# Sums of the down projection's weights: made in DRAM by a queue of transfers instead of in SBUF by the seven passes

## The chip, the cores and the metric

One core of a Trainium2 chip runs the whole program. The time is that of one execution on the device, in microseconds (us). Three timed runs of the kernel before gave 1393.69 us in the median (1390.49 to 1396.89). The profile is of one further execution.

## The reference, cut to what matters

Two layers of a diffusion backbone work on 640 tokens: 512 latent tokens (tiles 0 to 3) and 128 context tokens (tile 4). Each layer has a mixing half and a SwiGLU half. The change lies in the last matrix product of the SwiGLU half, and the instructions that it moves past lie in the mixing half.

```python
def swiglu(h, w_gate_up, w_down):
    g, u = jnp.split(h @ w_gate_up, 2, axis=-1)
    return (jax.nn.silu(g) * u) @ w_down            # w_down: 2816 x 1024, float32
...
q_nope, q_rope, ckv, k_rope = mla_project(pd, ...)  # rmsnorm of parts of pd, then q and kv
p = jax.nn.softmax(s * scale, axis=-1)              # per head, 4 heads
...
x = x + gate2 * rmsnorm(swiglu(h2, w_gate_up, w_down), g_post_ffn)
```

## The kernel before, in words

**Precision.** A float32 operand is split into a high part (`fp32r`, made by ACT) and the rest (made by DVE). A product takes three matmuls, L227 to L229. Each weight tile goes DRAM, `raw` (a pool of three buffers), ACT, DVE, `w` (a pool of eight).

**The down projection.** `w_down` runs one level of a seven-product scheme: the inner dimension is halved (e = 0, 1) and so are the output columns (h = 0, 1). Four blocks of weights, each 2816 x 1024 / 4, and three sums of them are needed. Each block comes in six groups g: five of 512 KB and one of 256 KB. The seven passes stand in the order p1, p2, p5, p6, p3, p7, p4, and each goes over the six groups. In the kernel before, p1 loads block (0,0) into buffers `V` and uses it, then POOL issues an accumulating transfer that adds block (0,1) to `V` in SBUF (L1079), so that p5 finds a sum there; p5 adds a further block for p6, p6 one for p4, and p7 adds two blocks in a `raw` buffer. So each layer has 24 loads by SP (L1076, L1083) and 24 accumulating transfers by POOL.

**The order.** Program order is written out with a planner: `clk` counts estimated matmul time, `bg` is a list of steps that are put between matmuls at a given spacing, and `spawn`ed tasks wait a stated time. After that, a scheduler takes the program and puts the instructions of each engine in an order of its own: what is free of dependences may be moved far ahead of its place in the program. On the chip each engine works through its own order, one instruction after the other; a wait holds all that is queued behind it on that engine.

**POOL in the mixing half.** POOL has small jobs that others need: the reciprocal root of every rmsnorm (`rsq`: `rs` at L248/L250, `rt` at L252). For `pd_chain`, DVE multiplies `pdt` by `rt` (L696), TensorE transposes `pdt` (L240), and the results feed queries and keys. In `keys`, POOL writes the rotary rows of `kT` (L744, L745). In `scores`, POOL scales the probabilities of every second head, `P` (L810), and TensorE then transposes `P` (L240). `ada_sum` adds up modulation sums with matmuls (L346), copies them by ACT to `s`, waits a planned time, and transposes `s` (L240).

Of the kernel before, what the change touches and what calls it, by code (L numbers as in the profile page):

```python
# [131 lines left out]
class Trunk:  # L132
# [227 lines left out]
    def queue_ada_v(self, l, r):  # L360
# [5 lines left out]
        def step(half, k):  # L366
# [11 lines left out]
            if k == 7:  # L378
                self.spawn(self.ada_sum(mod, mc, half, acc, 1.10), 5.66)
# [665 lines left out]
    def w_down(self, l, src, hid, gg, nxt):  # L1045
# [13 lines left out]
        V = [None] * 3  # L1059
# [10 lines left out]
        def vg(g):  # L1070
            return V[g // 2][:, (g % 2) * 1024 : (g % 2) * 1024 + cnt(g) * 512]

        def into(g, e, h):
            if V[g // 2] is None:
                V[g // 2] = self.W()
            nc.sync.dma_start(out=vg(g), in_=dram(e, h, g))  # L1076

        def add(dst, e, h, g):
            nc.gpsimd.dma_start(out=dst, in_=dram(e, h, g), accum_op=ALU.add)  # L1079

        def fresh(g, e, h):
            r = self.raw()[:, 0 : cnt(g) * 512]
            nc.sync.dma_start(out=r, in_=dram(e, h, g))  # L1083
            return r

        def wsplit(g, s):
            w = self.wp.tile([128, 2, 1024], R, tag="w", name=self.nm("w"))
            n = cnt(g) * 512
            self.split(w[:, 0, :n], w[:, 1, :n], s)
            return w  # L1090
# [17 lines left out]
        def run(make, outs, tail=0, first=None, then=None):  # L1108


            kept = []
            for g in range(NG):
                h, w = first if first and g == 0 else make(g)
# [61 lines left out]
        def p1(g):  # L1175
            into(g, 0, 0)
            w = wsplit(g, vg(g))
            add(vg(g), 0, 1, g)
            h = xsplit(g, [x(g, 0)[:, :, A4]])
            self.tt(d(g), x(g, 1)[:, :, D4], x(g, 0)[:, :, D4], ALU.subtract)  # L1180
            return h, w
# [6 lines left out]
        def p2(g):  # L1188
            w = wsplit(g, fresh(g, 1, 0))
# [14 lines left out]
        def p5(g):  # L1204
            w = wsplit(g, vg(g))
            add(vg(g), 1, 1, g)
# [6 lines left out]
        def p6(g):  # L1213
            w = wsplit(g, vg(g))
            add(vg(g), 1, 0, g)
# [9 lines left out]
        def p3(g):  # L1225
            w = wsplit(g, fresh(g, 1, 1))
# [9 lines left out]
        def p7(g):  # L1236
            r = fresh(g, 0, 1)
            add(r, 1, 1, g)
            w = wsplit(g, r)
# [8 lines left out]
        def p4(g):  # L1248
            return xsplit(g, [x(g, 1)[:, :, B4]]), wsplit(g, vg(g))
# [91 lines left out]
    def run(self):  # L1341
# [4 lines left out]
        for l in range(L):  # L1346
# [9 lines left out]
            nxt = None  # L1356
            if l + 1 < L:
                mod1, q = self.queue_ada_w(l + 1, 0)
                self.bg, self.bg_last = [(6.6, f) for f in q], self.now + 12.0
# [7 lines left out]
            pre = self.w_down(l, x, hid, gg, nxt)  # L1367
# [42 lines left out]
```

## Time and profile before

| | |
|---|---|
| median of three runs | 1393.69 us |
| profiled execution | 1388.35 us, of which the span is 1386.5 us |
| PE busy | 1336.1 us (96%) |
| DVE / ACT / POOL busy | 1023.8 / 692.4 / 152.8 us |
| DMA | 203.68 MB: 179.25 MB by SP's queue (q1), 23.07 MB by POOL's (q0) |

A busy PE is not PE at its peak, since matmuls overlap; what an engine waits for says more. A row of the timeline has a start in us, a duration in us, the engine, the line, the operation with output and inputs, the number of instructions merged, and in brackets the idle time before it with what ended it.

### The profile page before, as it was taken

The page shows a single profiled execution, that of the slowest core. Times are in us where ns is not written, and L with a number is a line of the kernel's source. Part 1 is how long each engine was busy: PE and PEld are TensorE (multiplying, and loading weights), DVE is VectorE, ACT ScalarE, POOL GpSimd, SP SyncE. Part 2 cuts the span into 40 slices and gives each one's busy share as a digit, 9 for nine tenths or more (in the row PEclk, how much of TensorE's full clock was granted, in tenths as well). Part 3 has the DMA queues.
Part 4 walks back from the last instruction along what each step waited for, and adds up shares of the span by engine and source line. Part 5 has one row for each costly group of instructions (what it writes and reads, how often), then busy time and mean ns, then how long its engine had stood idle before and what let it go on. Part 6 is the DMA issues. An engine that isn't in the chain of part 4 may idle for free.

```text
span 1386.5 us, 21414 instructions
## 1 busy us (share of the span) xinstructions
PE 1336.1 (96%) x8188; PEld 1202.3 (87%) x8188; DVE 1023.8 (74%) x1794; ACT 692.4 (50%) x1398; POOL 152.8 (11%) x186
## 2 busy tenths in 40 slices
PE   5899999999999999999899899999999999999996
PEld 2789978899999999888688798778999999998885
DVE  3789476599988985777788956757977777665956
ACT  4543275565544454455673324746644444444734
POOL 1101121110000000121221101302000000010220
PEclk9999999999999999999999999999999999999999
DMA  9555247243333333778565623553223222365983
GB/s 374 170 178 185 89 140 245 104 169 108 122 122 107 122 121 125 176 143 193 171 213 170 197 88 122 175 207 123 76 92 92 80 88 77 107 177 126 184 200 119
DMA packets 57974, 203.68 MB, mean 147 GB/s; under 512 B 7488, under 2 KB 8384, under 8 KB 56848
## 3 DMA queue, kind: packets, MB, share of 16 engines
q1 hardware_dynamic: 50960, 179.25, 38.9%
q0 software_dynamic: 6912, 23.07, 9.5%
q8 instruction: 64, 1.05, 0.3%
q14 instruction: 38, 0.31, 0.1%
HBM read 191.61 MB, written 10.68 MB: 146 GB/s over the span
## 4 chain that ended last, share of the span: by engine, by line
PE 73%; DMA 9%; DVE 7%; issue 5%; ACT 3%; POOL 1%; POOLq 0%; DVEq 0%; ACTq 0%; SPq 0%
PE ps L227 23%; PE ps L229 22%; PE ps L228 22%; DMA raw<-in_w_dn 4%; PE ps L240 3%; DVE w L217 2%; DVE acc L377 2%; DMA raw<-in_ada 2%; PE ps L284 2%; ACT w L211 1%; DMA raw<-in_w_out 1%; PE ps L829 1%; POOL rt L252 1%; DMA raw<-in_w_s 1%; POOL rs L250 1%
## 5 line engine op out<-in xcount | busy, mean ns | idle before, releaser
L217 DVE TENSOR_TENSOR w<-raw,w 128x512 fp32r<-128x512 f32 (+2 forms) x220 | 198.0, 905 | 99.9 <-ACT w L211 98.6
L211 ACT ACTIVATE w<-raw 128x512 fp32r<-128x512 f32 (+2 forms) x220 | 175.5, 801 | 179.0 <-PE ps L229 82.2
L227 PE MATMUL ps<-T,w 128*128 128x320 f32 x640 | 198.5, 310 | 0.0
L229 PE MATMUL ps<-T,w 128*128 128x320 f32 x640 | 197.8, 309 | 0.0
L228 PE MATMUL ps<-T,w 128*128 128x320 f32 x640 | 197.7, 309 | 0.0
L227 PE MATMUL ps<-b,w 128*128 128x320 f32 x608 | 188.1, 309 | 0.0
L228 PE MATMUL ps<-b,w 128*128 128x320 f32 x608 | 187.9, 309 | 0.0
L229 PE MATMUL ps<-b,w 128*128 128x320 f32 x608 | 187.9, 309 | 0.0
L227 PE MATMUL ps<-w,hs 128*128 128x512 f32 x396 | 156.4, 395 | 8.0 <-ACT hs L211 6.7
L229 PE MATMUL ps<-w,hs 128*128 128x512 f32 x396 | 155.5, 393 | 3.0 <-DVE hs L217 3.0
L228 PE MATMUL ps<-w,hs 128*128 128x512 f32 x396 | 155.3, 392 | 0.0
L211 ACT ACTIVATE w<-sw 128x512 fp32r<-128x512 f32 x160 | 96.3, 625 | 77.4 <-PE ps L229 65.3
L211 ACT ACTIVATE s<-ps 128x320 f32<-128x320 f32 (+2 forms) x148 | 65.3, 442 | 126.6 <-PE ps L229 106.2
L214 DVE TENSOR_TENSOR s<-ps,s 128x320 f32<-128x320 f32 (+1 forms) x144 | 68.5, 481 | 75.7 <-PE ps L229 75.4
L227 PEld LDWEIGHTS ps<-T,w 128*128 128x128 f32 x640 | 120.1, 188 | 2.1 <-issue 1.7
L228 PEld LDWEIGHTS ps<-T,w 128*128 128x128 f32 x640 | 120.1, 188 | 0.0
L229 PEld LDWEIGHTS ps<-T,w 128*128 128x128 f32 x640 | 120.1, 188 | 0.0
L227 PEld LDWEIGHTS ps<-b,w 128*128 128x128 f32 x608 | 114.1, 188 | 0.4 <-ACT s L211 0.3
L228 PEld LDWEIGHTS ps<-b,w 128*128 128x128 f32 x608 | 114.1, 188 | 0.1
L229 PEld LDWEIGHTS ps<-b,w 128*128 128x128 f32 x608 | 114.1, 188 | 0.0
L217 DVE TENSOR_TENSOR w<-sw,w 128x512 fp32r<-128x512 f32 x160 | 106.0, 684 | 5.1 <-ACT w L211 3.2
L227 PEld LDWEIGHTS ps<-w,hs 128*128 128x128 f32 x396 | 75.1, 190 | 25.3 <-ACT hs L211 8.0
(236 smaller groups left out, 2848.0 us busy)
## 6 DMA issues: line engine op xcount, KB each, us to landing
raw<-in_w_gu SPq DMA_DIRECT2D x88, 512.0 KB, 3.5
raw<-in_ada SPq DMA_DIRECT2D x64, 512.0 KB, 4.5
raw<-in_w_dn SPq DMA_DIRECT2D x30, 512.0 KB, 3.6
wk<-in_w_dn POOLq DMA_DIRECT2D x30, 512.0 KB, 5.6
ada<-in_ada SPq DMA_DIRECT2D x8, 1024.0 KB, 15.5
raw<-in_w_out SPq DMA_DIRECT2D x16, 512.0 KB, 4.1
wk<-in_ada SPq DMA_DIRECT2D x8, 1024.0 KB
xs<-work SPq DMA_DIRECT2D x15, 512.0 KB, 4.8
```

Source lines behind the costliest of these rows:

```text
L211: self.nc.scalar.activation(out, in_, f, **kw)
L214: self.nc.vector.tensor_tensor(out, x, y, op=op)
L217: self.nc.vector.tensor_tensor(lo, src, hi.bitcast(F32), op=ALU.subtract)
L227: mm(out, lh, rh, start=start, stop=False, skip_group_check=more)
L228: mm(out, lh, rl, start=False, stop=False, skip_group_check=more)
L229: mm(out, ll, rh, start=False, stop=stop, skip_group_check=more)
L240: self.nc.tensor.transpose(out, in_, self.ident)
L250: self.nc.gpsimd.tensor_scalar(r, ms, EPS, None, op0=ALU.add)
L252: self.nc.gpsimd.tensor_tensor(r2, r, self.mhalf[:, :n], op=ALU.pow)
L284: self.nc.tensor.matmul(ps[32 * j : 32 * j + 32, :], self.cond[:, k, :], s, start=start, stop=stop, tile_position=(0, 32 * j))
L377: nc.vector.scalar_tensor_tensor(acc[:, s], raw, c, acc[:, s], op0=ALU.mult, op1=ALU.add)
L829: self.nc.tensor.matmul(ps[64 * e : 64 * e + 64, :], lhs[e], rhs[e], start=start, stop=stop, tile_position=(0, 64 * e))
```

## The change

A new function, `queue_sums`, makes four arrays `v[0]` to `v[3]` of sums per layer in DRAM. POOL issues all of it: 12 copies of weights DRAM to DRAM, 12 accumulating transfers on these, then six copies and six accumulating transfers for `v[1]`, and six and six for `v[3]`: 48 transfers per layer, 96 in all. The steps go into `bg` beside gate and up, spaced over 210 us of planner time. The seven passes load what they need with SP from the weights or from `v`, through `raw`, 42 loads per layer; `run` now makes the operands of group g + 1 before the matmuls of group g. Besides, `ada_sum` in the mixing half plans 6.0 us in place of 1.10 us before its transposes.

```diff
@@ -376,7 +376,7 @@
                 else:
                     nc.vector.scalar_tensor_tensor(acc[:, s], raw, c, acc[:, s], op0=ALU.mult, op1=ALU.add)
             if k == 7:
-                self.spawn(self.ada_sum(mod, mc, half, acc, 1.10), 5.66)
+                self.spawn(self.ada_sum(mod, mc, half, acc, 6.0), 5.66)
 
         return mod, [lambda h=h, k=k: step(h, k) for h in range(2) for k in range(8)]
 
@@ -1042,7 +1042,34 @@
             fast(j, cur, prep(j + 1, ops) if j + 1 < NJ else None)
         return hid
-    def w_down(self, l, src, hid, gg, nxt):
+    def queue_sums(self, l):
+        nc, a = self.nc, self.a
+        v = [[self.dp.tile([128, 1040], F32, tag=f"v{i}{g}", name=self.nm("v"))[:, 0 : (2 if g < 5 else 1) * 512] for g in range(6)] for i in range(4)]
+        def dram(e, h, g):
+            return a["w_dn"][l, e, h, g] if g < 5 else a["w_dt"][l, e, h]
+        def copy(i, g, s):
+            nc.gpsimd.dma_start(out=v[i][g], in_=s)
+        def add(i, e, h, g):
+            nc.gpsimd.dma_start(out=v[i][g], in_=dram(e, h, g), accum_op=ALU.add)
+        todo = []
+        for g in range(6):
+            todo.append(lambda g=g: [copy(0, g, dram(0, 0, g)), copy(2, g, dram(0, 1, g))])
+        for g in range(6):
+            todo.append(lambda g=g: [add(0, 0, 1, g), add(2, 1, 1, g)])
+        for i, (e, h) in ((1, (1, 1)), (3, (1, 0))):
+            for g in range(6):
+                todo.append(lambda g=g, i=i: copy(i, g, v[0 if i == 1 else 1][g]))
+            for g in range(6):
+                todo.append(lambda g=g, i=i, e=e, h=h: add(i, e, h, g))
+        return v, todo
+    def w_down(self, l, src, hid, gg, vs, nxt):
@@ -1067,23 +1093,9 @@
         def dram(e, h, g):
             return a["w_dn"][l, e, h, g] if g < 5 else a["w_dt"][l, e, h]
-        def vg(g):
-            return V[g // 2][:, (g % 2) * 1024 : (g % 2) * 1024 + cnt(g) * 512]
-
-        def into(g, e, h):
-            if V[g // 2] is None:
-                V[g // 2] = self.W()
-            nc.sync.dma_start(out=vg(g), in_=dram(e, h, g))
-
-        def add(dst, e, h, g):
-            nc.gpsimd.dma_start(out=dst, in_=dram(e, h, g), accum_op=ALU.add)
-
-        def fresh(g, e, h):
-            r = self.raw()[:, 0 : cnt(g) * 512]
-            nc.sync.dma_start(out=r, in_=dram(e, h, g))
-            return r
-
-        def wsplit(g, s):
+        def wsplit(g, src):
+            s = self.raw()[:, 0 : cnt(g) * 512]
+            nc.sync.dma_start(out=s, in_=src)
             w = self.wp.tile([128, 2, 1024], R, tag="w", name=self.nm("w"))
             n = cnt(g) * 512
             self.split(w[:, 0, :n], w[:, 1, :n], s)
@@ -1108,9 +1120,10 @@
         def run(make, outs, tail=0, first=None, then=None):
-            kept = []
+            kept, ready = [], first or make(0)
             for g in range(NG):
-                h, w = first if first and g == 0 else make(g)
+                h, w = ready
+                ready = make(g + 1) if g + 1 < NG else None
                 if g >= NG - tail:
                     kept.append((g, h, w))
                 else:
@@ -1173,9 +1186,7 @@
         b4 = [self.PS(), None]
         def p1(g):
-            into(g, 0, 0)
-            w = wsplit(g, vg(g))
-            add(vg(g), 0, 1, g)
+            w = wsplit(g, dram(0, 0, g))
             h = xsplit(g, [x(g, 0)[:, :, A4]])
             self.tt(d(g), x(g, 1)[:, :, D4], x(g, 0)[:, :, D4], ALU.subtract)
             return h, w
@@ -1186,7 +1197,7 @@
         later.append(lambda: [self.act(cc[:, 0, p, :], bA[p]) for p in range(2)])
         def p2(g):
-            w = wsplit(g, fresh(g, 1, 0))
+            w = wsplit(g, dram(1, 0, g))
             return xsplit(g, [x(g, 1)[:, :, A4]]), w
         go(p2, [(bC[0], 0, True, True), (bC[1], 128, True, True), (b4[0], 256, False, True)])
@@ -1202,8 +1213,7 @@
         later.extend(lambda t=t: left(t) for t in (0, 1, 4))
         def p5(g):
-            w = wsplit(g, vg(g))
-            add(vg(g), 1, 1, g)
+            w = wsplit(g, vs[0][g])
             return xsplit(g, [d(g)[:, :, 128:384]]), w
         go(p5, [(bB[0], 0, True, True), (bB[1], 128, True, True)])
@@ -1211,8 +1221,7 @@
         later.append(lambda: [self.act(cc[:, 1, p, :], bB[p]) for p in range(2)])
         def p6(g):
-            w = wsplit(g, vg(g))
-            add(vg(g), 1, 0, g)
+            w = wsplit(g, vs[1][g])
             s = d(g)[:, :, 128:384]
             nc.vector.scalar_tensor_tensor(s, s, -1.0, x(g, 0)[:, :, 0:256], op0=ALU.mult, op1=ALU.subtract)
             return xsplit(g, [s]), w
...
@@ -1234,9 +1243,7 @@
         later.extend(lambda p=p: end(p) for p in range(2))
         def p7(g):
-            r = fresh(g, 0, 1)
-            add(r, 1, 1, g)
-            w = wsplit(g, r)
+            w = wsplit(g, vs[2][g])
             h = self.Q([2, 2, 384], R, "hs")
             k = cnt(g)
             s = self.S()[:, 0 : k * 256].rearrange("p (k n) -> p k n", k=k)
@@ -1246,7 +1253,7 @@
             return h, w
         def p4(g):
-            return xsplit(g, [x(g, 1)[:, :, B4]]), wsplit(g, vg(g))
+            return xsplit(g, [x(g, 1)[:, :, B4]]), wsplit(g, vs[3][g])
         early = []
         steps = run(p7, [(bA[0], 0, None, True), (bA[1], 128, None, True), (b4[1], 256, False, True)], 2, None, lambda: early.append(p4(0)))
@@ -1354,9 +1361,11 @@
             x = self.dp.tile([NT, 128, D], F32, tag="xs", name=self.nm("xs"))
             pre = self.w_out(l, src, x, ys, gg, mod2, last)
             nxt = None
+            vs, qs = self.queue_sums(l)
             if l + 1 < L:
                 mod1, q = self.queue_ada_w(l + 1, 0)
-                self.bg, self.bg_last = [(6.6, f) for f in q], self.now + 12.0
+                qs = [x for k in range(max(len(q), len(qs))) for x in (*q[k : k + 1], *qs[k : k + 1])]
+            self.bg, self.bg_last = [(210.0 / len(qs), f) for f in qs], self.now + 12.0
             hid = self.gate_up(l, pre)
             self.drain_bg()
             gg = self.gates(gate, 1)
@@ -1364,7 +1373,7 @@
                 h = self.new_h()
                 src = self.dp.tile([NT, 128, D], F32, tag="xs", name=self.nm("xs"))
                 nxt = (mod1, h, src)
-            pre = self.w_down(l, x, hid, gg, nxt)
+            pre = self.w_down(l, x, hid, gg, vs, nxt)
             if l + 1 < L:
                 self.more_pd(l + 1)
                 self.mixer_start(l + 1)```

The instruction order shows where the scheduler puts all this. With n = 0 to 95 counted along POOL, transfers 0 to 47 belong to layer 0 and 48 to 95 to layer 1. `DMASW0` to `DMASW7` are the semaphores of POOL's transfers: transfer n raises number n mod 8. All 96 stand in POOL's order ahead of the first `P` scaling of layer 0. The first eight wait for nothing and stand first of all; later ones wait for a transfer issued six to eight places earlier.

POOL in layer 0, kernel before: the last two rmsnorms of `pd_chain` (`ms_544`, `ms_607`), then `kT_1249` and `kT_1250` (the rotary key rows) and the first `P`.

```order
L250 TENSOR_SCALAR rs_551<-ms_544 128x2 [waits Activation_49]
L252 TENSOR_TENSOR rt_553<-rs_551,mhalf 128x2 [waits Pool_49]
L250 TENSOR_SCALAR rs_611<-ms_607 128x2 [waits Activation_49]
L252 TENSOR_TENSOR rt_613<-rs_611,mhalf 128x2 [waits DVE_49,Pool_49]
L744 CAST kT_1249<-krT_283 64x640 [waits DVE_49,PE_49,Pool_49]
L744 CAST kT_1249<-krT_283 64x640
L745 TENSOR_TENSOR kT_1249<-krT_283,kT_1249 64x640 [waits Pool_49] x2
L744 CAST kT_1250<-krT_283 64x640 [waits DMAHW4_49,PE_49]
L744 CAST kT_1250<-krT_283 64x640
L745 TENSOR_TENSOR kT_1250<-krT_283,kT_1250 64x640 [waits Pool_49] x2
L560 COPY krT_6974<-ctx_6970 128x128 [waits DMAHW6_49,Pool_49]
L810 TENSOR_SCALAR P_1610<-P_1610,ri_1680 128x640 [waits DVE_49,Activation_49]
```

POOL in the changed kernel at the same rmsnorms; L1055 is a copy and L1058 an accumulating transfer, `v_28..` is layer 0 and `v_95..`, `v_96..` layer 1.

```order
L1058 DMA v_2867<-in_w_dn 128x1024 [waits DMASW6_49]
L250 TENSOR_SCALAR rs_551<-ms_544 128x2 [waits Activation_49]
L1058 DMA v_2868<-in_w_dn 128x1024 [waits DMASW7_49]
L252 TENSOR_TENSOR rt_553<-rs_551,mhalf 128x2 [waits Pool_49]
L1058 DMA v_2869<-in_w_dn 128x1024 [waits DMASW0_49]
L1058 DMA v_2870<-in_w_dt 128x512 [waits DMASW1_49]
L250 TENSOR_SCALAR rs_611<-ms_607 128x2 [waits Activation_49]
L1055 DMA v_9591<-in_w_dn 128x1024
L252 TENSOR_TENSOR rt_613<-rs_611,mhalf 128x2 [waits DVE_49,Pool_49]
```

The add into `v_2870` is transfer 47, and its wait on `DMASW1` is for transfer 41, the copy that it adds to. So `rt_613` now stands behind the landing of transfers 0 to 41, which are 24 copies and 18 accumulating transfers.

POOL in the changed kernel from the last transfers of layer 1 to the first `P`.

```order
L1055 DMA v_9614<-v_9602 128x512 [waits DMASW3_49]
L1058 DMA v_9609<-in_w_dn 128x1024 [waits DMASW4_49]
L1058 DMA v_9610<-in_w_dn 128x1024 [waits DMASW5_49]
L1058 DMA v_9611<-in_w_dn 128x1024 [waits DMASW6_49]
L1058 DMA v_9612<-in_w_dn 128x1024 [waits DMASW7_49]
L1058 DMA v_9613<-in_w_dn 128x1024 [waits DMASW0_49]
L1058 DMA v_9614<-in_w_dt 128x512 [waits DMASW1_49]
L744 CAST kT_1250<-krT_283 64x640 [waits DMAHW4_49,PE_49]
L744 CAST kT_1250<-krT_283 64x640
L745 TENSOR_TENSOR kT_1250<-krT_283,kT_1250 64x640 [waits Pool_49] x2
L560 COPY krT_7061<-ctx_7057 128x128 [waits DMAHW6_49,Pool_49]
L810 TENSOR_SCALAR P_1610<-P_1610,ri_1680 128x640 [waits DVE_49,Activation_49]
```

The copy into `v_9614` is transfer 89 and the add into it transfer 95. `kT_1250` and `P_1610` stand behind the landing of transfers 0 to 89, which are 48 copies and 42 accumulating transfers; `kT_1249` stands a little further ahead, behind transfer 79.

PE in layer 1, kernel before: the transposes of `s_7745`, the modulation sums that ACT copies out after the matmuls at L346, stand 11 matmuls behind those. The last eight of the 11 and what follows:

```order
L227 MATMUL ps_7722<-h_5789,w_7718 128x320
L228 MATMUL ps_7722<-h_5790,w_7718 128x320
L229 MATMUL ps_7722<-h_5789,w_7718 128x320
L227 MATMUL ps_7721<-h_5789,w_7718 128x320
L228 MATMUL ps_7721<-h_5790,w_7718 128x320
L229 MATMUL ps_7721<-h_5789,w_7718 128x320
L227 MATMUL ps_7722<-h_5789,w_7718 128x320
L228 MATMUL ps_7722<-h_5790,w_7718 128x320
L240 MATMUL ps_7756<-ident,s_7745 128x128 x4
L229 MATMUL ps_7722<-h_5789,w_7718 128x320
```

In the changed kernel the same transposes (of `s_7832`) stand 48 matmuls behind.

```order
L227 MATMUL ps_7809<-h_5863,w_7805 128x320
L228 MATMUL ps_7809<-h_5864,w_7805 128x320
L229 MATMUL ps_7809<-h_5863,w_7805 128x320
L240 MATMUL ps_7895<-ident,s_7832 128x128 x4
L227 MATMUL ps_7909<-h_5861,w_7906 128x320
```

They moved by 37 matmuls. The number of matmuls, and of ACT and DVE splits, is the same in both kernels.

## Rows read from the trace of the kernel before

**Rows 1.** The page: busy time and share of the span of each engine.
```profile
PE 1336.1 (96%) x8188; PEld 1202.3 (87%) x8188; DVE 1023.8 (74%) x1794; ACT 692.4 (50%) x1398; POOL 152.8 (11%) x186
```

**Rows 2.** Who PE waited for, 672 to 700 us: total, times, longest (us).
```profile
PE ps L227 <- ACT hs L211: 4.3, 1, 4.3
PE ps L229 <- DVE hs L217: 2.6, 3, 0.9
```

**Rows 3.** Who PE waited for, 1320 to 1386 us.
```profile
PE ps L227 <- ACT hs L211: 2.3, 1, 2.3
PE ps L227 <- ACT cc L211: 1.3, 1, 1.3
PE ps L229 <- DVE hs L217: 0.5, 1, 0.5
```

**Rows 4.** Who PE waited for, 720 to 870 us.
```profile
PE ps L240 <- ACT s L211: 6.0, 1, 6.0
```

**Rows 5.** Timeline of POOL, whole span: start, duration, operation.
```profile
12.40 0.57 POOL L252 TENSOR_TENSOR rt<-rs,mhalf 128x1 f32<-128x1 f32 x1
...
70.61 0.71 POOL L252 TENSOR_TENSOR rt<-rs,mhalf 128x2 f32<-128x2 f32 x1
...
161.29 1.49 POOL L744 CAST kT<-krT 64x640 fp32r<-64x640 f32 x2 [42.60 <-PE ps L228]
162.85 3.19 POOL L745 TENSOR_TENSOR kT<-krT,kT 64x640 fp32r<-64x640 f32 x2
166.11 0.29 POOL L560 COPY krT<-ctx 128x128 f32<-128x128 f32 x1
180.43 1.90 POOL L810 TENSOR_SCALAR P<-P,ri 128x640 f32<-128x640 f32 x1 [14.03 <-ACT V L211]
...
1340.95 0.87 POOL L1079 DMA_DIRECT2D raw<-in_w_dn  x1 [4.24 <-DMA raw<-in_w_dn]
1341.91 1.04 POOL L248 TENSOR_SCALAR rs<-mso 128x1 f32<-128x1 f32 x1
```

**Rows 6.** Timeline of all engines, 186 to 190 us: the first transposes of P.
```profile
188.76 1.25 PE L240 MATMUL ps<-ident,P 128*128 128x128 f32 x10
```

**Rows 7.** Who POOL waited for: total, times, longest (us).
```profile
POOL raw L1079 <- DMA raw<-in_w_dn: 39.9, 6, 14.6
```

**Rows 8.** DMA queues, 598 to 618 us: packets, MB, share of 16 engines.
```profile
q0 software_dynamic: 686, 2.55, 77.1%
```

**Rows 9.** DMA queues, 20 to 40 us.
```profile
q1 hardware_dynamic: 2130, 8.17, 101.9%
```

**Rows 10.** Windows: length, busy time (instructions) of each engine, granted clock, DMA share, GB/s.
```profile
0.00:71.00 71.00, 51.17 (x280) 34.93 (x281) 38.60 (x96) 34.15 (x83) 10.84 (x25) 1.00 0.70 266
71.00:180.00 109.00, 107.24 (x693) 95.94 (x692) 79.60 (x124) 39.96 (x79) 11.92 (x10) 1.00 0.47 152
0.00:180.00 180.00, 158.41 (x971) 130.87 (x972) 118.20 (x220) 74.11 (x162) 22.75 (x34) 1.00 0.56 197
```

**Rows 11.** Windows around the wait of rows 4.
```profile
795.00:800.00 5.00, 3.20 (x13) 3.20 (x14) 4.22 (x7) 1.54 (x2) 0.00 (x0) 0.50 0.74 226
800.00:810.00 10.00, 10.00 (x72) 10.00 (x71) 8.09 (x11) 3.24 (x6) 0.00 (x0) 0.98 0.53 179
```

More of the change, by code (lines that the diff above doesn't have):

```diff
@@ L1058, in w_down @@
         dd = [self.Q([3, 2, 384], F32, "dd") for _ in range(2)]
-        V = [None] * 3
         def x(g, e):
@@ L1225, in p3 @@
         def p3(g):
-            w = wsplit(g, fresh(g, 1, 1))
+            w = wsplit(g, dram(1, 1, g))
             s = d(g)[:, :, 128:384]
```

## The prediction, made before the changed kernel ran

> **What bounds the kernel now.** I read the page's busy times first: PE is busy 96% of the span [rows 1], so what can still be won is small, and what counts is what makes PE wait. Then I read who PE waited for in the two stretches of the down projection that have any such row: 6.9 us in layer 0 and 4.1 us in layer 1 [rows 2, 3], 11.0 us together. All else that the seven passes wait for lies beside matmuls. A third list holds one wait of 6.0 us for the modulation sums of layer 1 [rows 4]. Last comes POOL's timeline [rows 5]. POOL is idle most of the time, and for that reason its work is early: the last `rt` of layer 0's `pd_chain` is done at 71.3 us, `kT_1250` at 166.0, the first `P` at 182.3, and PE transposes that `P` at 188.76 [rows 6]. This is the schedule that the change touches, since the instruction order puts all 96 transfers ahead of that `P`.
>
> **What a wait on POOL does.** In the old down projection POOL stood 39.9 us in six waits for a load on which an accumulating transfer depended [rows 7]. After a wait of 4.24 us of that kind the transfer was issued at 1340.95, and the next `rs` followed at 1341.91, though nothing ties it to the transfer [rows 5]. So a transfer that waits holds the rmsnorms behind it.
>
> **Price of one transfer.** The mean size is (5 x 512 + 256) / 6 KB = 0.4806 MB. With POOL's queue alone at work, accumulating transfers moved 2.55 MB in 77.1% of 20 us, or 15.4 us [rows 8]: 165 GB/s, 2.91 us for the mean. SP's loads, back to back, moved 8.17 MB in 20.4 us of share [rows 9]: 401 GB/s, 1.20 us. An accumulating transfer in DRAM I price at 2.91 us, the row that it is nearest to; it cannot be under 2.40 (two streams read at 401 GB/s), it is 4.11 if reading the destination in DRAM costs a whole load on top (2.91 + 1.20), and 5.31 if writing it there costs as much again. A copy DRAM to DRAM is in no row. It reads one stream, as a load does, and writes to DRAM; it lies between 1.20 (a load) and 2.91 (an accumulation, which does all that a copy does and more). I take the middle, 2.05.
>
> The Trainium skill (DMA: Bandwidth & Descriptors, section on latency and other measured facts) gives 207 to 214 GB/s per direction for copies between HBM tensors. By it, a copy would be 2.29 us as an estimate, and the sum below 11.5 us longer. No row here shows it.
>
> **What else runs on the engines.** Up to 180 us the kernel moves 197 GB/s x 180 us = 35.5 MB, of it 266 x 71 = 18.9 MB in the first 71 us [rows 10]. At 401 GB/s that is 88 us, and 47 us of these in the first 71. In rows 9 the loads alone filled 101.9% of the 16 engines, so nothing is free beside them. I add the loads and the new transfers.
>
> The Trainium skill (same page, section "Issuing engines are not separate DMA queues") has it that transfers from SP and POOL end up on the same 16 engines and interleave. By that rule they add up; were the queues independent, the sum would lose the 88 us. Rows 9 agree as far as they go, since one queue alone fills all 16. The other way is the second rival.
>
> **The sum.** `rt_613` stands behind transfers 0 to 41, 24 copies and 18 accumulations: 47 + 24 x 2.05 + 18 x 2.91 = 149 us against 71. DVE's product with it, and behind that the weight splits, the loads and PE, all wait. `P_1610` stands behind 0 to 89, 48 copies and 42 accumulations: 88 + 48 x 2.05 + 42 x 2.91 = 88 + 98.4 + 122.2 = 308.6 us. Behind that come `kT_1250` (1.49 + 3.19), a copy (0.29) and `P` itself (1.90) [rows 5], 6.9 us: 315.5 us. PE wanted it at 188.76, so PE is 126.7 us late. The compute between these two points, 110 us, is shorter than the 160 us of transfers that lie there, so POOL still sets the end. From there on both kernels do the same work.
> - The issues themselves, 0.87 us each [rows 5], 90 of them 78 us, lie inside the 308.6 us of moving. Were the transfers quicker than the issues they would be the bound; they are not, at 1.20 us or more.
> - The clock: after the wait of 6.0 us PE had the lower level, 0.50 granted, over 5.0 us with 3.20 us busy [rows 11], which is 1.6 us lost at least. A long stall should end so too, at up to 5 us; I take 3. Restarts before the last are covered by POOL's lateness.
> - The down projection: 48 accumulating transfers in two layers go, and with them what PE waits for there: at most 11.0 us; some of these waits are for activations (`cc`, `hs`), not weights. I take 6, from 0 to 11. SP's 18 more loads per layer lie beside the passes at 1.20 us of engine time each, in place of 24 accumulations at 2.91.
> - The later transposes of `s`: 37 matmuls more ahead of them at 10 / 72 = 0.139 us [rows 11] hide 5.1 of the 6.0 us [rows 4]. I take 5, from 0 to 7.6 with the lower clock.
> - Splits, matmuls and evacuations are as many as before: 0. The lookahead by one group has eight `w` buffers for two in use; were it short of them, a pass would wait as now.
>
> 126.7 + 3 - 6 - 5 = 118.7 us. Against the profiled execution, 1388.35 + 118.7 = 1507 us; this stood 5.3 us under the median of the runs, 1393.69, so I forecast 1512 us.
>
> **Bounds.** Low prices: 88 + 48 x 1.20 + 42 x 2.40 = 246, so with the 6.9 and less 188.8 PE is 64 us late; less 18.6 for the gains at their most, nothing for the clock: 1439 us. High prices: 88 + 48 x 2.91 + 42 x 5.31 = 451, 269 us late, 5 for the clock, no gains: 1668 us; both at their highest together is unlikely.
>
> **Rivals.**
> 1. Both kinds are dearer in DRAM: a copy 2.91 us, an accumulation 4.11, since the destination is read from DRAM too, where before it lay in SBUF. For it: no row shows such a transfer. Against: in rows 8 the engines' own share, 77.1%, went with the low rate, so that reading two streams may already be the bound. 88 + 139.7 + 172.6 = 400, and 400 + 6.9 - 188.8 + 3 - 11 = 210 us: 1604 us.
> 2. The loads and POOL's transfers do not slow each other. For it: before 180 us the engines are 56% busy [rows 10], so there are gaps. Against: rows 9. Then 220.6 + 6.9 - 188.8 + 3 - 11 = 31 us: 1424 us.
> 3. The other side: POOL's chain is never late, the transfers being spread over a time in which POOL has nothing to do, and the gains remain. This decides at the first gate: 42 transfers in 70 us, or 1.67 us each, and 90 in 182 us, 2.02 us each, with nothing taken from the loads. The mean at my prices is 2.45 us; at the lowest it is 1.76 for the 90. Then 1388.35 + 5.3 - 11 = 1383 us. For it: POOL is busy 11% [rows 1].
> 4. The change doesn't do what it says. It speaks of gate and up; the instruction order has the transfers at the start of the program. That is no rival but the ground of the forecast; were they issued where they are written, rival 3's time would come out.
>
> **Chances.** Forecast 0.66, rival 1 0.15, rival 2 0.13, rival 3 (with 4) 0.06. The range, 1420 to 1640 us, takes in the low bound, rival 1, rival 2 and the high bound but for its last 28 us; it leaves out rival 3. This kernel's measurement can tell about 0.5%, or 7 us, from no change. Faster by more than that 0.04 (most of rival 3), within it 0.02, slower 0.94.
>
> **What the profile would show.** If I am right, PE's waits for DVE's `pdt` and for `kT` or `P` hold some 120 us before the end of layer 0's mixing, and POOL's longest waits are for DMA in the first 300 us; the DMA share there is near 1; the last `rt` of `pd_chain` comes at about 150 us and the first `P` of layer 0 at about 315; from there to the end it is as long as before, less about 11 us. The waits of rows 2 to 4 shrink. I am wrong in the price if the 96 transfers are through at 180 us or at 450; wrong in the mechanism if `P_1610` comes near 182 us, or if the lost time lies in the down projections.

## The result, and the profile after

The changed kernel took 1467.67 us in the median of four runs (1467.47 to 1469.24), the kernel before 1394.46 (four runs): a ratio of 1.052, 95% interval 1.0497 to 1.0543, slower. The forecast was 1512 us, so its direction and its place held, and its size was 44 us too long. The profiled execution took 1469.24 us. In two of the experiments below one run of four was slow (e5_half 1527.83 us, e10_early_copies 7500.69); their medians are of all four, 0.1 to 0.2 us above those of the fast runs, and ratios are of fast runs alone.

The page of the changed kernel, which answers to [rows 1]: busy time, then the granted clock and DMA share in 40 slices, then the two queues (packets, MB, share of 16 engines).

```profile
PE 1352.7 (92%) x8188; PEld 1219.8 (83%) x8188; DVE 1024.3 (70%) x1794; ACT 692.0 (47%) x1398; POOL 173.8 (12%) x234
...
PEclk9778879999999999999999999999999999999999
DMA  9999999563443343335556453355322222334553
...
q1 hardware_dynamic: 56144, 196.55, 40.3%
q0 software_dynamic: 13312, 46.14, 12.2%
```

All that is odd stands in the first seven slices, 257 us: DMA full, the granted clock down to 0.7. Windows of the changed kernel (columns as in [rows 10]) say the same in numbers: before, the engines were 0.70 and 0.47 busy in the first two.

```profile
0.00:71.00 71.00, 28.33 (x136) 14.86 (x136) 14.88 (x38) 17.52 (x32) 19.50 (x36) 0.89 1.00 337
71.00:180.00 109.00, 69.54 (x343) 60.71 (x343) 50.70 (x94) 29.73 (x77) 36.77 (x56) 0.83 1.04 302
180.00:260.00 80.00, 63.09 (x385) 59.43 (x386) 40.72 (x59) 17.92 (x34) 28.07 (x36) 0.82 1.02 273
260.00:300.00 40.00, 39.97 (x287) 31.65 (x287) 27.95 (x92) 24.28 (x71) 11.43 (x8) 1.00 0.49 159
```

POOL's timeline in the changed kernel, at the last rmsnorms of `pd_chain`, at `kT` and at the first `P`, answers to [rows 5].

```profile
101.81 0.23 POOL L250 TENSOR_SCALAR rs<-ms 128x2 f32<-128x2 f32 x1
104.66 0.90 POOL L1058 DMA_DIRECT2D v<-in_w_dt  x1 [2.62 <-issue]
105.27 1.05 POOL L252 TENSOR_TENSOR rt<-rs,mhalf 128x2 f32<-128x2 f32 x1
...
134.96 0.74 POOL L252 TENSOR_TENSOR rt<-rs,mhalf 128x2 f32<-128x2 f32 x1
...
228.53 1.49 POOL L744 CAST kT<-krT 64x640 fp32r<-64x640 f32 x2
...
257.48 1.49 POOL L744 CAST kT<-krT 64x640 fp32r<-64x640 f32 x2 [2.33 <-PE ps L228]
...
277.13 1.90 POOL L810 TENSOR_SCALAR P<-P,ri 128x640 f32<-128x640 f32 x1 [14.54 <-ACT V L211]
```

An `rs` is done at 102.04, but its `rt` follows at 105.27, since POOL stood idle for 2.62 us before a transfer between them, with which `rt` has nothing to do. The last `rt` comes at 134.96 instead of 70.61, the first `P` at 277.13 instead of 180.43. Who PE waited for in the first 290 us, the five longest of nine rows with 98.9 us together; none of the nine is for `kT` or `P`, and in the first 300 us of the kernel before the row of `pdt` had 1.8 us and that of `ada` 11.2:

```profile
PE ps L240 <- DVE pdt L696: 19.2, 4, 9.7
PE ps L240 <- ACT s L211: 18.0, 3, 13.4
PE ps L240 <- issue: 15.0, 1, 15.0
PE ps L228 <- DVE U L217: 11.6, 2, 6.9
PE ps L284 <- DMA ada<-in_ada: 10.9, 2, 9.2
```

And POOL's longest waits, 0 to 300 us. "issue" means that the profile names no releaser; L1058 are the accumulating transfers.

```profile
POOL v L1058 <- issue: 122.7, 42, 6.2
```

PE's waits in 808 to 958 us, the stretch of [rows 4], are below. In 761 to 789 and 1401 to 1468 us, the stretches of [rows 2, 3], no wait is listed any more.

```profile
PE ps L227 <- DVE ua L724: 2.7, 1, 2.7
PE ps L240 <- DVE work L438: 1.9, 1, 1.9
```

To see where each kernel wins or loses, I cut every span at four points of DVE's timeline: the start of its first and its last product into `hid` (the end of a step of gate and up) in either layer. Times in us; "middle" is layer 0's `w_down` and layer 1's mixing half, "end" is layer 1's `w_down`.

| | head | gate, up 0 | middle | gate, up 1 | end | span |
|---|---|---|---|---|---|---|
| before | 291.9 | 244.0 | 435.0 | 242.6 | 173.1 | 1386.5 |
| changed | 388.4 | 246.8 | 422.9 | 242.5 | 166.9 | 1467.5 |
| e2_none | 296.2 | 247.0 | 419.9 | 242.7 | 166.7 | 1372.5 |
| e1_paced | 297.7 | 256.5 | 422.1 | 248.5 | 166.9 | 1391.8 |
| e1_burst | 294.4 | 272.1 | 419.7 | 263.3 | 166.8 | 1416.4 |
| e7_copies | 294.2 | 255.3 | 419.8 | 242.6 | 166.8 | 1378.6 |
| e8_spread | 294.9 | 258.0 | 436.4 | 242.5 | 167.6 | 1399.4 |
| e6_small | 353.5 | 246.7 | 422.6 | 242.5 | 166.4 | 1431.7 |
| e4_mid | 379.3 | 247.9 | 420.8 | 242.6 | 166.7 | 1457.3 |
| e5_half | 359.3 | 245.7 | 420.5 | 242.5 | 166.8 | 1434.9 |
| e11_half_mid | 331.6 | 245.6 | 419.4 | 242.5 | 167.0 | 1406.2 |
| e10_early_copies | 365.4 | 246.1 | 422.8 | 242.5 | 166.7 | 1443.5 |
| e9_second | 294.6 | 245.7 | 429.1 | 244.2 | 166.9 | 1380.5 |

The changed kernel loses 96.5 us in the head and 2.8 in layer 0's gate and up (e2_none loses 3.0 there too, without a transfer; why stays open), and wins 12.1 and 6.2 us in the two stretches with a `w_down`.

### The profile page after: what moved, and what is told of

Same layout as the page of the kernel before. It is cut to its first block, busy times and chain, and to the rows that moved or that the text cites. A ratio compares the mean times of both kernels' runs of the same rounds, so it can differ in the third digit from the quotient of the medians.

```text
span 1467.5 us, 21508 instructions
## 1 busy us (share of the span) xinstructions
PE 1352.7 (92%) x8188; PEld 1219.8 (83%) x8188; DVE 1024.3 (70%) x1794; ACT 692.0 (47%) x1398; POOL 173.8 (12%) x234
## 2 busy tenths in 40 slices
DMA  9999999563443343335556453355322222334553
## 3 DMA queue, kind: packets, MB, share of 16 engines
q1 hardware_dynamic: 56144, 196.55, 40.3%
q0 software_dynamic: 13312, 46.14, 12.2%
q8 instruction: 64, 1.05, 0.3%
## 4 chain that ended last, share of the span: by engine, by line
issue 64%; PE 16%; DMA 9%; DVE 5%; POOL 4%; ACT 1%; SPq 0%; POOLq 0%; DVEq 0%; ACTq 0%
DMA raw<-in_ada 5%; PE ps L227 4%; PE ps L228 4%; PE ps L229 4%; DVE acc L377 2%; PE ps L240 2%; POOL rt L252 2%; PE ps L284 1%; DMA raw<-in_w_pd 1%; POOL v L1058 1%; DVE w L217 1%; PE ps L829 1%; DMA raw<-in_w_out 1%; POOL rs L250 1%; POOL rs L248 1%
## 5 line engine op out<-in xcount | busy, mean ns | idle before, releaser
L217 DVE TENSOR_TENSOR w<-raw,w 128x1024 fp32r<-128x1024 f32 (+2 forms) x268 | 252.4, 947 | 119.4 <-ACT w L211 118.0
L211 ACT ACTIVATE w<-raw 128x1024 fp32r<-128x1024 f32 (+2 forms) x268 | 222.2, 832 | 190.8 <-DMA raw<-in_w_b 71.2
L227 PE MATMUL ps<-T,w 128*128 128x320 f32 x640 | 198.7, 310 | 1.4 <-ACT s L211 1.2
L228 PE MATMUL ps<-T,w 128*128 128x320 f32 x640 | 197.8, 309 | 0.0
L229 PE MATMUL ps<-T,w 128*128 128x320 f32 x640 | 197.7, 309 | 0.0
L227 PE MATMUL ps<-b,w 128*128 128x320 f32 x608 | 188.4, 310 | 0.1
L229 PE MATMUL ps<-b,w 128*128 128x320 f32 x608 | 187.9, 309 | 0.0
L228 PE MATMUL ps<-b,w 128*128 128x320 f32 x608 | 187.8, 309 | 0.0
L227 PE MATMUL ps<-w,hs 128*128 128x512 f32 x396 | 154.4, 390 | 0.1
L228 PE MATMUL ps<-w,hs 128*128 128x512 f32 x396 | 154.1, 389 | 0.0
L229 PE MATMUL ps<-w,hs 128*128 128x512 f32 x396 | 153.9, 389 | 0.0
L211 ACT ACTIVATE w<-sw 128x512 fp32r<-128x512 f32 x160 | 96.0, 624 | 76.9 <-PE ps L229 64.6
L211 ACT ACTIVATE s<-ps 128x320 f32<-128x320 f32 (+2 forms) x148 | 65.2, 442 | 124.0 <-PE ps L229 100.4
L227 PEld LDWEIGHTS ps<-T,w 128*128 128x128 f32 x640 | 120.1, 188 | 4.0 <-ACT s L211 2.4
L214 DVE TENSOR_TENSOR s<-ps,s 128x320 f32<-128x320 f32 (+1 forms) x144 | 68.7, 483 | 78.0 <-PE ps L229 77.7
L228 PEld LDWEIGHTS ps<-T,w 128*128 128x128 f32 x640 | 120.1, 188 | 0.0
L229 PEld LDWEIGHTS ps<-T,w 128*128 128x128 f32 x640 | 120.1, 188 | 0.0
L227 PEld LDWEIGHTS ps<-b,w 128*128 128x128 f32 x608 | 114.1, 188 | 1.4 <-issue 0.8
L228 PEld LDWEIGHTS ps<-b,w 128*128 128x128 f32 x608 | 114.1, 188 | 0.1
L229 PEld LDWEIGHTS ps<-b,w 128*128 128x128 f32 x608 | 114.1, 188 | 0.0
L248 POOL TENSOR_SCALAR rs<-mso 128x1 f32<-128x1 f32 x20 | 10.0, 500 | 878.6 <-ACT work L211 878.5
L217 DVE TENSOR_TENSOR w<-sw,w 128x512 fp32r<-128x512 f32 x160 | 106.1, 685 | 5.3 <-ACT w L211 3.3
## 6 DMA issues: line engine op xcount, KB each, us to landing
raw<-in_w_gu SPq DMA_DIRECT2D x88, 512.0 KB, 3.6
raw<-in_ada SPq DMA_DIRECT2D x64, 512.0 KB, 6.6
v<-in_w_dn POOLq DMA_DIRECT2D x60, 512.0 KB, 10.8
raw<-v SPq DMA_DIRECT2D x40, 512.0 KB, 3.5
raw<-in_w_dn SPq DMA_DIRECT2D x30, 512.0 KB, 3.5
v<-v POOLq DMA_DIRECT2D x20, 512.0 KB, 9.4
raw<-in_w_out SPq DMA_DIRECT2D x16, 512.0 KB, 3.8
```

Source lines behind the costliest of these rows:

```text
L211: self.nc.scalar.activation(out, in_, f, **kw)
L214: self.nc.vector.tensor_tensor(out, x, y, op=op)
L217: self.nc.vector.tensor_tensor(lo, src, hi.bitcast(F32), op=ALU.subtract)
L227: mm(out, lh, rh, start=start, stop=False, skip_group_check=more)
L228: mm(out, lh, rl, start=False, stop=False, skip_group_check=more)
L229: mm(out, ll, rh, start=False, stop=stop, skip_group_check=more)
```

## Experiments

The kernel before was run again beside the experiments, with medians of 1393.1 to 1395.5 us; ratios are against it. Theory 1: the loss is in the head alone; the transfers add to the loads there, and POOL's order passes the delay on.

**Is it the place?** Each transfer is held behind the matmul recorded last where the program writes it (e1_paced), or all of a layer behind `w_out` (e1_burst); e2_none has none.

```diff
-            nc.gpsimd.dma_start(out=v[i][g], in_=s)
+            self.hold(nc.gpsimd.dma_start(out=v[i][g], in_=s), self.mark)   # e1_burst: start, taken at the head of queue_sums
```

> The changed kernel, with each of the 96 transfers that make the sums held behind the matmul last recorded where the planner puts it, so that they run through gate and up, and the head of the program has none. Theory 1 (loads and transfers share the DMA engines' time, and GpSimd's queue stands behind them; both only in the first 280 us): the 97 us by which the first P is late go, the 15 to 16 us that come back afterwards (97 us at P, 81 at the end) stay, 1394.5 - 15.7 = 1379 us, 1375 to 1387. Rival A (the delay comes from GpSimd's waits in its order alone): also 1379 here, since no work of the mixer stands behind a transfer. Rival C (the transfers' 180 us of engine time are paid wherever they run, by the loads of gate and up): no faster than before, 1394 or more.

> As the run with paced transfers, but all 48 transfers of a layer are held behind the last matmul of w_out, so that they run back to back at the start of gate and up, some 90 us for each layer. Theory 1: the 90 us of transfers and the loads of gate and up lie in a stretch where the engines were busy for a quarter to a half before, 1379 us, at most 5 us more where a burst and the loads together come to over 1.0; the rest as in the paced one. Rival C: 20 us or more above the paced one, since the loads of gate's first passes stand in the burst.

> The changed kernel without any of the 96 transfers: the four passes that load a sum load a plain block of the weights instead, so the sums are left out of the computation, and everything else stays. It is the floor. Theory 1: 1379 us, within 3 us of the paced one, since the transfers there are hidden; the first P stands where it stood before (180 us, within 3). If the transfers cost something in gate and up, this run is below the paced one by that. If the 15.7 us that came back after the first P came from elsewhere (later work having more slack because it started late), this run is at 1390 to 1395.

Measured: 1397.37 us (1.0013, 0.9992 to 1.0034), 1419.69 (1.0183) and 1375.61 (0.9862). The floor is 3 us under what was expected. All 92 us between it and the changed kernel hang on the transfers, and out of the head they cost 22 (paced) or 44 (burst). But 22 is not 0: theory 1 had said 1379. "In the head alone" fell, and rival A's 1379 with it. Rival C's numbers came true (1394 or more, the burst 20 or more above the paced run), though the price is 22 us and not 180. DMA queues in 350 to 400 us, e1_paced (accumulating transfers in pairs): queue rows as in [rows 8]; issue rows end with KB each and median us to landing.

```profile
q0 software_dynamic: 1734, 5.78, 61.4%
q1 hardware_dynamic: 1409, 5.24, 32.1%
...
raw<-in_w_gu SPq DMA_DIRECT2D x8, 512.0 KB, 9.9
```

The same stretch, e2_none:

```profile
q1 hardware_dynamic: 1696, 6.29, 36.6%
...
raw<-in_w_gu SPq DMA_DIRECT2D x8, 512.0 KB, 4.4
```

A weight load lands after 9.9 us instead of 4.4, later than it is needed. Who DVE waited for in 330 to 540 us of e1_paced (e2_none has 4.4 and 2.7 us in these rows), and who PE waited for in 275 to 540:

```profile
DVE sw L214 <- DMA raw<-in_w_gu: 10.1, 8, 2.5
...
DVE acc L410 <- DMA wk<-in_ada: 5.6, 2, 4.3
```

```profile
PE ps L227 <- DVE s L214: 6.4, 3, 3.7
```

In e2_none that row has 0.4 us. So PE waits for a DVE that had itself waited for loads.

**Is it the accumulating?** e7_copies drops it; e8_spread sends single transfers, layer 1's from layer 0's gate and up on.

```diff
-..., in_=dram(e, h, g), accum_op=ALU.add), self.mark)
+..., in_=dram(e, h, g)), self.mark)
```

```diff
+        if self.trk and self.now - self.trk_last >= self.trk[0][0]:   # in mm3; 5.2 us in layer 0, 13.0 us in layer 1
+            self.trk_last = self.now
+            self.hold(self.trk.pop(0)[1](), last.ins.name)
```

> The run with paced transfers (1397.4 us), with each of the 48 accumulating transfers made a plain copy of the same bytes, so that the sums are not sums; the count, the order and the holds stay. Theory 2, formed from the paced run (gate and up lost 9.5 us in layer 0 and 5.9 in layer 1 against the run without transfers, and in layer 0 nearly all of it in 350 to 400 and 442 to 488 us, where accumulating transfers ran, none where copies ran): the loss goes with the accumulations, about 1378 us, 1375 to 1383. Rival D (a load is delayed by any transfer of these bytes): the loss stays, or falls only in the ratio of the engines' time (1.2 us for a copy, 2.2 for an accumulation), 1388 to 1397.

> The changed kernel with all 96 transfers made one at a time behind matmuls: layer 0's one in 5.2 us of gate and up, layer 1's one in 13 us from there to layer 1's gate and up. It tries for the gain without the price. By theory 2 an accumulation alone delays a load by about its own 2.2 us, which a stretch with a load every 3.5 us has little slack for, and layer 1's accumulations come at half the rate: some 6 to 9 us of loss in layer 0, 2 to 5 in layer 1, 1383 to 1391 us. If no place is free of it, 1397 as the paced one; if spreading is all it needs, 1376 to 1380.

Measured: 1382.01 us (0.992, 0.9892 to 0.9948) and 1398.66 (1.0033). Theory 2 is half right. In layer 1 the loss was the accumulations': 248.5 us with them, 242.6 with copies. Windows of 1016 to 1056 us in e1_paced, where they come in pairs, and then of e7_copies:

```profile
1016.00:1056.00 40.00, 36.07 (x240) 35.54 (x239) 25.55 (x47) 17.16 (x35) 7.77 (x10) 0.98 0.87 209
```

```profile
1016.00:1056.00 40.00, 40.00 (x275) 40.00 (x274) 30.59 (x55) 20.36 (x42) 6.23 (x12) 1.00 0.69 235
```

In layer 0, where loads of 1 MB for the modulation run beside gate and up, copies cost 8.3 of the 9.5 us that the paced sums cost: there the theory fell. And e8_spread lost 11.0 us in layer 0's gate and up and 16.5 in the middle, where 24 of layer 1's transfers and the last seven of layer 0's run; 1383 to 1391 us in all had been expected. Thin spreading does not make them free; PE's listed waits in that middle (14 us, 6 in e2_none) show only half of the loss.

**What in the head costs?** e6_small cuts the transfers to 128 columns; e4_mid holds all 96 behind the mixer's first product, so that the head's rmsnorms stand in front of them.

```diff
-            nc.gpsimd.dma_start(out=v[i][g], in_=dram(e, h, g), accum_op=ALU.add)
+            nc.gpsimd.dma_start(out=v[i][g][:, 0:128], in_=dram(e, h, g)[:, 0:128], accum_op=ALU.add)   # e6_small
+            self.hold(nc.gpsimd.dma_start(out=v[i][g], in_=dram(e, h, g), accum_op=ALU.add), start)   # e4_mid: start = self.mark0
```

> The changed kernel with its 96 transfers where they were, at the program's head, each cut to 128 columns (a quarter of the bytes of the short blocks, an eighth of the others); the four passes load plain blocks, so the sums are left out. Count, issue instructions, order and waits stay. Theory 1 (the engines' time of loads and transfers adds up, and GpSimd's queue only passes that on): the transfers' 180 us of engine time fall to 25 to 45 us, part of it in the open first 71 us: 1385 to 1415 us. Rival A (GpSimd's waits in its order, whatever the bytes): 60 us or more of the 91 between the changed kernel and the one without transfers stay, 1435 to 1468.

> The changed kernel with all 96 transfers held behind the last matmul of the first product of layer 0's mixer (some 75 us in), so that no rmsnorm of the first stretch stands behind one; kT, P and what follows still do. Theory 1: from there on loads and transfers add up; some 60 transfers (36 copies at 1.2 us, 24 accumulations at 2.2) stand ahead of the first P's division: 75 + 50 us of loads + 96 = 221 us instead of 180, and the other 36 (67 us) run beside w_out's loads (0.49 of the engines) and cost 15 to 50 more: 1430 to 1475 us. Rival A (the cost is the 64 us by which the rmsnorms of the head stood behind transfers): 1375 + 97 - 64 = 1408 us or less.

Measured: 1433.51 us (1.0282) and 1461.57 (1.0487). The first lies between the two ranges, 1.5 us under rival A's; the second lies in theory 1's. POOL's timeline in e6_small, and two windows of it:

```profile
26.74 0.81 POOL L1058 DMA_DIRECT2D v<-in_w_dn  x1 [2.46 <-issue]
29.64 0.81 POOL L1058 DMA_DIRECT2D v<-in_w_dn  x1 [2.09 <-issue]
...
70.43 0.81 POOL L1058 DMA_DIRECT2D v<-in_w_dt  x1 [0.53 <-issue]
...
114.55 0.23 POOL L250 TENSOR_SCALAR rs<-ms 128x2 f32<-128x2 f32 x1
...
130.71 0.71 POOL L252 TENSOR_TENSOR rt<-rs,mhalf 128x2 f32<-128x2 f32 x1
...
240.09 1.90 POOL L810 TENSOR_SCALAR P<-P,ri 128x640 f32<-128x640 f32 x1 [13.98 <-ACT V L211]
```

```profile
0.00:71.00 71.00, 26.37 (x136) 13.02 (x136) 15.19 (x39) 18.00 (x34) 38.08 (x63) 0.98 0.85 262
71.00:120.00 49.00, 18.03 (x96) 16.58 (x97) 13.85 (x33) 12.16 (x29) 35.66 (x54) 0.69 0.62 107
```

With the engines at 0.62, the `rt` is as late as in the changed kernel: here POOL's own pace is the bound. But the order did not stay, as the expectation had it: all 96 transfers stand ahead of the head's last five rmsnorms in this kernel, where 49 stand ahead of the last `rt` in the changed one. Up to 114 us their issues take 70 us and the waits before them 42. Layer 0's 48 were all issued by 71 us (the row at 70.43), and the five rmsnorms took 17 us (114.55 to 131.42); with only these 48 ahead the last `rt` would have come at about 88 us, an estimate, and not at 131. So e6_small does not show that POOL's pace alone makes the changed kernel's loss. In e4_mid the engines are full from 120 us on:

```profile
75.00:120.00 45.00, 40.83 (x228) 36.28 (x228) 31.54 (x36) 12.94 (x24) 8.22 (x14) 0.94 0.81 291
120.00:300.00 180.00, 131.71 (x875) 106.27 (x874) 85.80 (x188) 59.28 (x143) 72.11 (x85) 0.88 1.03 279
300.00:340.00 40.00, 29.93 (x104) 22.08 (x105) 13.04 (x21) 10.37 (x21) 13.55 (x22) 0.81 1.05 302
```

But `kT` and `P` still stand behind transfers there, and the first row of PE's waits in 0 to 400 us is for POOL's `P`:

```profile
PE ps L240 <- POOL P L812: 32.4, 6, 16.8
```

So e4_mid shows that the head's rmsnorms are not the only place where POOL's order costs time; it does not speak against the order.

**How do the two share the 92 us?** e5_half leaves out layer 1's transfers; e11_half_mid holds layer 0's as e4_mid did; e10_early_copies has no accumulation.

```diff
+        if l == 1:                                # e5_half, e11_half_mid
+            return v, [lambda: None] * 36
-            nc.gpsimd.dma_start(out=v[i][g], in_=dram(e, h, g), accum_op=ALU.add)
+            nc.gpsimd.dma_start(out=v[i][g], in_=dram(e, h, g))          # e10_early_copies
```

> The changed kernel with only layer 0's 48 transfers, where they were (24 copies, 24 accumulations, all ahead of the rmsnorms of the head on GpSimd); layer 1's passes load plain blocks, so its sums are left out. The runs with small transfers (1433.5 us) and with held ones (1461.6) say that either cause alone costs most of it: GpSimd's order (the last rmsnorm of the head at 131 us with an eighth of the bytes, 135 in the changed kernel, 71 before) and the engines' time (1.03 and more from 120 us on with the rmsnorms in front). By the order alone this run has the same 48 transfers ahead of that rmsnorm, 60 us late, and 1375.6 + 60 = 1436 us, 1428 to 1443. By the engines' time alone, 48 transfers are 80 us beside the 100 us of loads that the first 180 us hold, so nearly all fits: 1376 to 1390.

> The changed kernel with its 48 accumulations at the head made plain copies of the same bytes, so the sums are not sums; count, order and waits stay. By the prices read from the changed kernel's queue (1.2 us for a copy, 2.2 for an accumulation) 42 to 48 us of engine time go, half of them ahead of the head's last rmsnorm, which comes at about 111 instead of 135 us: 1420 to 1443 us. If the landing waits of the chains set GpSimd's pace, whatever a transfer costs, 1455 to 1468.

> The run with only layer 0's 48 transfers (1438.1 us; layer 1's passes load plain blocks, so its sums are left out), with these held behind the last matmul of the mixer's first product, some 75 us in, so that the head's rmsnorms stand in front of them. If the 62 us of that run were the rmsnorms' place behind 48 transfers (last one at 135 us instead of 71), they go, and what is left is that the same 80 us of transfers now run beside the 50 us of loads from 75 us on, with the first P's division behind all 48: P at 75 + 50 + 80 = 205 us instead of 180, 1395 to 1408 us. If 48 transfers cost the head 60 us wherever they stand in it, 1436.

Measured: 1438.11 us (1.0299, 1.0276 to 1.0323), 1445.18 (1.0329, 1.0288 to 1.0369) and 1413.35 (1.0149, 1.013 to 1.0168). POOL in e5_half, then in e11_half_mid:

```profile
134.72 0.72 POOL L252 TENSOR_TENSOR rt<-rs,mhalf 128x2 f32<-128x2 f32 x1
...
245.54 1.90 POOL L810 TENSOR_SCALAR P<-P,ri 128x640 f32<-128x640 f32 x1 [14.00 <-ACT V L211]
```

```profile
69.94 0.71 POOL L252 TENSOR_TENSOR rt<-rs,mhalf 128x2 f32<-128x2 f32 x1
91.94 3.88 POOL L1061 DMA_DIRECT2D v<-in_w_dn  x7 [21.29 <-PE ps L229]
...
203.02 0.82 POOL L1064 DMA_DIRECT2D v<-in_w_dn  x1 [4.79 <-issue]
...
218.44 1.49 POOL L746 CAST kT<-krT 64x640 fp32r<-64x640 f32 x2
223.47 3.77 POOL L812 TENSOR_SCALAR P<-P,ri 128x640 f32<-128x640 f32 x2
```

So the account of the changed kernel is 1375.6 + 62.5 (layer 0's 48 transfers, by which the head's `rt` is 64 us late; nothing more is lost after that) + 29.6 (layer 1's 48, beside the loads from 135 to 255 us) = 1467.7. Putting the rmsnorms in front gave back 24.8 of the 62.5 us, less than expected: transfers and loads took 126 us, near the 130 worked out, but from 92 us on, when the matmul that held them ended, not from 75, and `kT` and `P` stand behind them. In e10_early_copies, with the count and the order kept, the last `rt` of the head came at 107.1 us (111 expected), 27.9 us earlier than in the changed kernel, and the time was 2 us above its range. A copy cost the engines 1.17 us less than an accumulation (worked out in the next section), and 24 x 1.17 = 28.1 us: with the order kept, the `rt` follows the engines' time.

**The edit of `ada_sum` alone.**

```diff
-                self.spawn(self.ada_sum(mod, mc, half, acc, 1.10), 5.66)
+                self.spawn(self.ada_sum(mod, mc, half, acc, 6.0), 5.66)
```

> The kernel before, with only the planner's cost of ada_sum changed as the change has it (1.10 to 6.0 us). Theory 1: the lag fell by 2.8 us across the stretch of layer 1's modulation sums in the changed kernel, so 1394.5 - 3 = 1391 to 1392 us. By the prediction's own term it is 5 us, 1389. If the edit does nothing by itself, 1394 to 1395.

Measured: 1390.65 us, 0.9979 (0.9958 to 0.9999), some 3 us, just told from nothing; the interval holds the prediction's 5 too.

**A version from what was found.** e9_second has the old `w_down` in layer 0, the new one in layer 1, with single transfers.

```diff
-            pre = self.w_down(l, x, hid, gg, vs, nxt)
+            pre = self.w_down(l, x, hid, gg, vs, nxt) if l else self.w_down_first(l, x, hid, gg, nxt)
+            if l:
+                vs, ts = self.queue_sums(l)
+                self.trk, self.trk_last = [(4.6, f) for f in ts], self.now
```

> A version made from what the runs showed: layer 0's w_down as in the kernel before, layer 1's as in the changed kernel, its 48 transfers one at a time in 4.6 us of the planner behind matmuls of layer 1's gate and up, and ada_sum at 6.0. In the paced run layer 1's gate and up lost time only where accumulations came in pairs (1016 to 1056 us), none where they came singly, and the stretch behind it was 6.3 us shorter in every run with the sums. Theory 2: the 3 us of ada_sum and the 6.3 us stay, at most 3 us are lost: 1384 to 1388 us. If single accumulations at this rate delay the loads as they did in layer 0: 1390 to 1396.

Measured: 1383.14 us (1382.33 to 1384.73), ratio 0.991, 0.9891 to 0.993: faster than both, and 0.9 us under the expected range. Its window where the engines are busiest in layer 1's gate and up shows PE losing 0.7 of 40 us:

```profile
1055.00:1095.00 40.00, 39.34 (x269) 39.05 (x268) 27.27 (x50) 18.83 (x39) 5.73 (x7) 1.00 0.78 172
```

## Why the prediction was right, and where its sizes were off

- **The mechanism held up to its last step.** The loss is in the head; from the first `P` to the end the changed kernel is faster (1190.4 us against 1206.1). The last `rt` came at 135 us (149 forecast), and layer 0's 48 transfers, which hold it back, cost 62 us (e5_half). But the forecast let POOL set the end, with some 120 us of PE's waits for `pdt`, `kT` or `P`: the profile has 19.2 us for `pdt` and no row for the other two. PE's lost time is spread over much that was late behind the rmsnorms and the loads. And where the forecast had POOL wait for DMA, its 122.7 us have no releaser in the profile.
- **Adding loads and transfers held**: the engines stand at 1.00 to 1.04 of their time up to 260 us, so rival 2 (1424 us) fell.
- **The price of a transfer was the term that was mis-sized.** POOL's queue took 8.5% of 1443.5 us for 96 copies in e10_early_copies, 1.28 us each (2.05 taken), and 12.2% of 1467.5 us in the changed kernel, so an accumulation 1.28 + (179.0 - 122.7) / 48 = 2.45 us (2.91 taken). Rival 1 (dearer in DRAM) fell with that. The sum by these prices is 88 + 48 x 1.28 + 42 x 2.45 = 252 us instead of 308.6, and the last add of the 96 was issued at 254.3. That it comes so near is in part luck: by 255 us 45.43 of POOL's 46.14 MB had moved, four or five transfers more than the 90 of the sum, with the engines at 1.02 to 1.04. At the first gate, too, 22.65 MB or 47 transfers had moved by 135 us, and not 42: 47 + 24 x 1.28 + 23 x 2.45 = 134 us. There the high price and the low count offset each other in the 149 us.
- **The chain behind `kT_1250` was left out.** I had `P` follow it in 6.9 us. But `P` needs the scores, and they need `kT`: 19.65 us from the start of one to the start of the other (257.48 to 277.13), 19.14 before. At `kT_1250` POOL waited 2.33 us for PE, so in the end late work through late loads ended last, and POOL's transfers only just not. Nor had I counted that PE takes up that `P` only 6.4 us after it is done, before (182.33 to 188.76) as now (279.03 to 285.4). These errors have the opposite sign: 126.7 - 53.5 (POOL through at 255.1 instead of 308.6) + 2.3 + 14.7 (the chain) + 6.4 = 96.6, against 96.5 us lost in the head. That the forecast came within 44 us is owed in part to this offset.
- **The gains were larger**: 12.1 + 6.2 = 18.3 us in place of 11, as the waits of [rows 2 to 4], 17.0 us, all went; `ada_sum` has about 3 of it. The new `run` also makes each group's operands one group earlier, and no run separates that from the sums. Layer 0's gate and up took 2.8 back. The 3 us for the clock are part of the 96.5 and not measured apart.
- **Sum of the misses**: 126.7 - 96.5 + 3 + 7.3 - 2.8 = 37.7 us, the distance from 1507 to the profiled 1469.2. The rest of the 44 is the 5.3 us that I added for the median; the changed kernel's profile stood 1.6 above its own.
- **The last line of rival 4 was wrong**: issued where they are written, the transfers do not give 1383 us but 1397 (e1_paced).

Left open: how the 62 us divide between POOL's own pace and the engines' time that its order passes on. The estimate from e6_small gives the pace alone some 15 us (88 against 73.0 in e2_none), and e10_early_copies speaks for the engines' time; no run has layer 0's 48 transfers made small in the changed kernel's order.

## What to carry to other kernels

A transfer without dependences may be issued at the program's start, whatever place the code gives it: look at the order, and hold it behind an instruction of the stretch that should hide it. A free share of the DMA engines does not yet hide a transfer: what counts is how soon the loads beside it are needed. Move only the sums whose transfers such a stretch has room for; here that was one layer of two.

## What the runs showed of the hardware

A copy DRAM to DRAM cost the engines about what a plain load does. DMA queues of the changed kernel, 5 to 24 us, copies beside loads:

```profile
q1 hardware_dynamic: 968, 4.60, 58.7%
q0 software_dynamic: 927, 3.35, 43.3%
```

That is 3.35 MB in 8.2 us of share, 407 GB/s, against 401 for loads in [rows 9]; over the 96 copies of e10_early_copies it was 376. The Trainium skill (DMA: Bandwidth & Descriptors, "Latency and other measured facts") gives 207 to 214 GB/s per direction for copies between HBM tensors in rows of 16 KiB, issued by SP or ACT, at row pitches of 512 KiB and of 4 MiB plus 4 KiB. The copies here have rows of 4 KB and are issued by POOL; for them this trace shows nearly twice as much, and the measurement decides.

An accumulation in DRAM cost less than one into SBUF. In 165 to 194 us of the changed kernel q0 holds only accumulations:

```profile
q0 software_dynamic: 1191, 4.33, 75.3%
```

That is 198 GB/s, 2.42 us for the mean transfer, against 165 in [rows 8]. The 2.2 us of the expectations came from 33 to 75 us, where 5.82 MB moved: more than the 5.5 MB of accumulations issued by then, so that copies were among them. Beside gate and up both kinds cost more: worked out as above, 1.46 us for a copy (e7_copies, 10.2% of 1378.6 us) and 2.83 for an accumulation (e1_paced, 14.8% of 1391.8).

With 64 KB instead of 512 KB in each, POOL still stood 2 to 2.5 us before an accumulation while loads filled the engines (e6_small, 23 to 38 us), a wait for which the profile names no one; with all the bytes it was 2.3 to 6.2 us (changed kernel, 38 to 70 us).
